# The first feed-forward of a streaming encoder layer by one level of Strassen's scheme

## The chip, the core and the metric

The kernel runs on one core of a Trainium2 chip. The metric is the device time of one launch in microseconds. TensorE (PE) multiplies matrices and writes its results to PSUM; VectorE (DVE) and ScalarE (ACT) read PSUM and SBUF; GpSimd (POOL) works on SBUF; SyncE (SP) issues nearly all DMA transfers between HBM and SBUF.

## The reference, cut

One layer of an encoder for 1024 + 64 = 1088 tokens of width 1024 (two groups of requests, same weights): feed-forward with half weight, token mixing (gated linear attention and stick-breaking attention), second feed-forward, with a layer norm after each. The change concerns the first line.

```python
D_MODEL, D_FF = 1024, 2816

def swiglu(x, w_in, w_out):
    gate, up = jnp.split(x @ w_in, 2, axis=-1)
    return (jax.nn.silu(gate) * up) @ w_out

h = layer_norm(DN_ALPHA * x + 0.5 * swiglu(x, ffn1_w_in, ffn1_w_out), ln1_g, ln1_b)
...
h = layer_norm(DN_ALPHA * h + mix, ln2_g, ln2_b)
y = layer_norm(DN_ALPHA * h + 0.5 * swiglu(h, ffn2_w_in, ffn2_w_out), ln3_g, ln3_b)
```

All is float32. A product is made as three matmuls of rounded operands: each operand is split into a high part (a cast) and a low part (what the cast left over), and high x high, high x low and low x high are summed in PSUM.

## The kernel before, in words

Activations lie transposed, features on the 128 partitions and tokens along the free axis. The tokens are cut into three chunks of 384, 384 and 320 (`CHUNKS`). The hidden width is 22 tiles of 128 (`NH`), the model width 8 (`KT`).

`stage` (L460 and after) loads x chunk by chunk, two feature tiles per DMA into `xt`, and splits it: ScalarE casts to `X0h`, `X1h`, `X2h` (L467), VectorE subtracts to `X0l` and so on (L468). `ffn` makes the feed-forward. Its `gate_up` takes one hidden tile and for each chunk makes the gate in a bank `mm` and the up product in a bank `up`, 24 matmuls each (`mm3`, L235 to L237); ScalarE applies silu (L314), VectorE multiplies by 0.5 and the up product (L315), ScalarE and VectorE split the result to `hh` and `hl` (L320, L321), which stay in SBUF, five tiles deep. After every four hidden tiles `out_tiles` multiplies them by the output weights (L366 to L368) and VectorE adds the bank to the accumulator `acc` in SBUF (L378; for the first four tiles L371 and L374 start it from x itself). Weights are loaded as 512 KB into `raw` (`wraw`, L173; `wtile`, L206; L347), cast by ScalarE into `wh` (L185) and subtracted by GpSimd into `wl` (L186). `first` puts the first hidden tiles between the loads of x; `middle` alternates four gate/up tiles and four output tiles; `last` keeps gate/up of tiles 18 to 21 and their output for the third chunk.

`layer_norm` (generator) works on a chunk: sums over the feature tiles on VectorE (L251 to L256), the mean by a matmul with `ones` into `st` (L247), differences (L261), squares (L263), the variance in the same way, a square root and a reciprocal (L275), then gain and bias (L277, L280). `norm_split` splits the result for the next matmuls (L291, L293). `finish1` is the norm of a chunk with its store to `d_h`. `weave(main, filler)` takes steps of `filler` (matmul work) between the steps of `main` for as many microseconds as `main` asks: the norms of chunks 0 and 1 are woven with `last`, that of chunk 2 with `gla_early`, the first products of the token mixing for chunks 0 and 1.

The order on each engine is made by the framework's planner from the program order and its own estimate of what is ready; an operation whose operands and buffers are free can move ahead of others. A pool of buffers that lands on the memory of a closed pool waits for all users of that pool. The only other pools in the way here are `hp` and `pf` (hidden tiles and banks of the feed-forward) and `xp`.

## Time and profile before

| what | value |
|---|---|
| median of 3 runs | 3009.25 us (3008.7 to 3011.52) |
| profiled execution, its own time | 3012.4 us |
| span of the profiled execution | 3010.7 us |
| mean granted TensorE clock | 0.993 |
| matmul instructions | 18444 |

The profile is one execution. A matmul's recorded length overlaps that of the next, so the rate of TensorE is read from the distance between starts. Busy shares are given for stretches of the span; the granted clock is 1.0 at the upper of its two levels (2.4 GHz) and 0.5 at the lower (1.2 GHz).

### The profile page before, as it was taken

How to read it: one execution, taken by the hardware profiler on the slowest of the kernel's cores; microseconds unless marked ns; L12 is line 12 of the kernel's file. 1: busy time of each engine (PE TensorE's matmuls, PEld its weight loads, DVE VectorE, ACT ScalarE, POOL GpSimd, SP SyncE). 2: the span in 40 equal slices, each digit the busy share in tenths (PEclk: the TensorE clock that was granted, in tenths of full speed). 3: DMA queues.
4: the chain of work that ended last, by engine and by line, in shares of the span. 5: the costliest groups of instructions: out<-in, count | busy, mean ns of one | idle time of the engine just before them, and what ended most of it. 6: DMA issues, size and time to landing. Idle time of an engine off the chain costs nothing. (4 is left out here: it accounts for less than half of the span.)

```text
span 3010.7 us, 43873 instructions
## 1 busy us (share of the span) xinstructions
PE 2941.7 (98%) x18444; PEld 2887.6 (96%) x18444; DVE 1077.2 (36%) x1715; ACT 885.1 (29%) x1721; POOL 895.1 (30%) x714
## 2 busy tenths in 40 slices
PE   8999999999899999999999999999799999999997
PEld 8999999999788999999999999999799999999997
DVE  2232121223845434334444444253842121212226
ACT  3111111111555433323333333222542111111125
POOL 3212212223632211122223222334754122122225
PEclk9999999999999999999999999999999999999998
DMA  4111111112423121221223223544432111111123
GB/s 138 47 38 50 46 46 42 44 52 61 133 69 71 39 57 54 80 77 51 82 55 91 70 71 105 168 129 133 131 103 85 43 50 38 55 43 42 44 84 109
DMA packets 217302, 220.06 MB, mean 73 GB/s; under 512 B 10160, under 2 KB 214704, under 8 KB 217104
## 3 DMA queue, kind: packets, MB, share of 16 engines
q1 hardware_dynamic: 203280, 199.42, 23.0%
q10 hardware_dynamic: 13824, 17.83, 1.6%
q8 instruction: 145, 2.38, 0.3%
q14 instruction: 53, 0.43, 0.0%
HBM read 180.52 MB, written 36.70 MB: 72 GB/s over the span
## 5 line engine op out<-in xcount | busy, mean ns | idle before, releaser
L186 POOL TENSOR_TENSOR wl<-raw,wh 128x512 fp32r<-128x512 f32 (+1 forms) x498 | 736.9, 1499 | 1760.7 <-ACT wh L185 1750.3
L185 ACT CAST wh<-raw 128x512 fp32r<-128x512 f32 (+1 forms) x498 | 321.5, 675 | 962.4 <-PE up L367 325.2
L315 DVE SCALAR_TENSOR_TENSOR sg<-sg,up 128x384 f32<-128x384 f32 (+1 forms) x132 | 70.2, 532 | 745.1 <-PE up L237 743.5
L235 PE MATMUL mm<-X0h,wh 128*128 128x384 f32 (+1 forms) x864 | 292.9, 339 | 10.8 <-ACT wh L185 10.7
L235 PE MATMUL mm<-X2h,wh 128*128 128x320 f32 (+1 forms) x928 | 296.1, 319 | 5.4 <-DVE g L1025 2.9
L237 PE MATMUL mm<-X2h,wl 128*128 128x320 f32 (+1 forms) x928 | 291.3, 314 | 2.1 <-POOL wl L186 2.1
L237 PE MATMUL mm<-X0h,wl 128*128 128x384 f32 (+1 forms) x864 | 289.5, 335 | 1.6 <-POOL wl L186 1.6
L236 PE MATMUL mm<-X2l,wh 128*128 128x320 f32 (+1 forms) x928 | 291.1, 314 | 0.0
L236 PE MATMUL mm<-X0l,wh 128*128 128x384 f32 (+1 forms) x864 | 289.3, 335 | 0.0
L235 PE MATMUL mm<-X1h,wh 128*128 128x384 f32 x800 | 272.6, 341 | 1.7 <-DVE qs L605 1.7
L237 PE MATMUL mm<-X1h,wl 128*128 128x384 f32 x800 | 268.1, 335 | 0.0
L236 PE MATMUL mm<-X1l,wh 128*128 128x384 f32 x800 | 268.1, 335 | 0.0
L235 PEld LDWEIGHTS mm<-X2h,wh 128*128 128x128 f32 x928 | 175.5, 189 | 8.2 <-ACT wh L185 3.6
L367 PE MATMUL mm<-hl,wh 128*128 128x384 f32 (+1 forms) x528 | 173.7, 329 | 6.0 <-DVE hl L321 6.0
L237 PEld LDWEIGHTS mm<-X2h,wl 128*128 128x128 f32 x928 | 175.3, 189 | 2.4 <-POOL wl L186 2.4
L235 PEld LDWEIGHTS mm<-X0h,wh 128*128 128x128 f32 x864 | 163.2, 189 | 14.2 <-ACT wh L185 11.0
L236 PEld LDWEIGHTS mm<-X2l,wh 128*128 128x128 f32 x928 | 175.6, 189 | 1.0
L368 PE MATMUL mm<-hh,wl 128*128 128x384 f32 (+1 forms) x528 | 173.6, 329 | 0.0
L366 PE MATMUL mm<-hh,wh 128*128 128x384 f32 (+1 forms) x528 | 173.5, 329 | 0.0
L367 PE MATMUL up<-hl,wh 128*128 128x384 f32 (+1 forms) x528 | 172.9, 328 | 0.2
L368 PE MATMUL up<-hh,wl 128*128 128x384 f32 (+1 forms) x528 | 172.9, 327 | 0.0
L366 PE MATMUL up<-hh,wh 128*128 128x384 f32 (+1 forms) x528 | 172.5, 327 | 0.0
(263 smaller groups left out, 6650.3 us busy)
## 6 DMA issues: line engine op xcount, KB each, us to landing
raw<-f_in SPq DMA_DIRECT2D x112, 512.0 KB, 3.6
raw<-w_in SPq DMA_DIRECT2D x70, 512.0 KB, 7.5
raw<-f_out SPq DMA_DIRECT2D x48, 512.0 KB, 4.1
raw<-w_ao SPq DMA_DIRECT2D x16, 512.0 KB, 4.0
raw<-w_bo SPq DMA_DIRECT2D x16, 512.0 KB, 3.7
raw<-w_o SPq DMA_DIRECT2D x16, 512.0 KB, 4.2
v_new<-v SPq DMA_DIRECT2D x4, 1024.0 KB, 4.7
xt<-x SPq DMA_DIRECT2D x8, 384.0 KB, 5.9
```

The lines of the kernel that those rows point to most:

```text
L185: nc.scalar.copy(oh, src)
L186: nc.gpsimd.tensor_tensor(ol, src, f32(oh), op=ALU.subtract)
L235: nc.tensor.matmul(ps[:, :w], wh[:, k, :], xh[:, k, :], start=(k == 0), stop=False)
L236: nc.tensor.matmul(ps[:, :w], wh[:, k, :], xl[:, k, :], start=False, stop=False)
L237: nc.tensor.matmul(ps[:, :w], wl[:, k, :], xh[:, k, :], start=False, stop=(k == KT - 1))
L315: nc.vector.scalar_tensor_tensor(sg, sg, 0.5, psu[:, :w], op0=ALU.mult, op1=ALU.mult)
L366: nc.tensor.matmul(ps[:, :w], wh[:, k, ms], hh, start=(k == 0), stop=False)
L367: nc.tensor.matmul(ps[:, :w], wh[:, k, ms], hl, start=False, stop=False)
L368: nc.tensor.matmul(ps[:, :w], wl[:, k, ms], hh, start=False, stop=(k == n - 1))
```

## The change

The first feed-forward is made with one level of Strassen's scheme in the form with seven products and fifteen sums. In the first half a product is (2 x 2 blocks of weights) by (2 x 2 blocks of x): the weights of one hidden tile are cut by gate/up and by the two halves of the model width; x is cut by those halves and by token halves. Tokens are now 4 x 272 (`HW`), two pairs `c`. For each hidden tile and pair `c` seven products of 4 x 3 matmuls of 272 columns take the place of eight. `weight_forms` makes the seven combined weights of a hidden tile (four sums on VectorE, seven casts on ScalarE, seven subtractions on GpSimd or VectorE), `token_forms` the seven combinations of x once at the start (`make_x`, on VectorE for the first pair, on GpSimd for the second); they stay in SBUF in `xa` and `xb`. The sums over products are made partly in PSUM (bank `qa` collects products 0, 2, 4, 5; `qb` the others) and partly at the evacuation.

The gated activations no longer stay in SBUF. After each pair of hidden tiles `hidden_forms` makes their seven combinations, splits them and stores them to HBM (`d_hc`, 557 KB each). When all 22 tiles are done, the buffers `p1` are closed, an accumulator for all tokens takes their place and is filled with x by four DMAs, and the output half runs over groups of hidden pairs (`GROUPS`), loading the combinations of a group into `xa` or `xb` while the other is used. The output is again seven products, each evacuated by VectorE into one block of the accumulator. The last group runs one token pair after the other; its last four steps are woven with the layer norm of tokens 0 to 543 (in parts of 384 and 160), and the norms of the parts 224 and 320 with the first products of the token mixing for chunk 0 alone. `gla_constants` come later, and the weights of the first feed-forward are laid out on the host so that each load is contiguous. Pools are opened later than before, and with `reuse_waits="tile"`: a tile waits for the users of earlier tiles on its own bytes alone.

The diff, cut to its core:

```diff
     def open_pool(name, **kw):
-        pool = tc.tile_pool(name=name, bufs=1, **kw)
+        pool = tc.tile_pool(name=name, bufs=1, reuse_waits="tile", **kw)
...
+    def weight_forms(A, n, pool, on_pool):
+        def form(src, i):
+            wh = pool.tile([P, 4, P], F32R, name="wh", tag="wh", bufs=7)[:, :n, :]
+            wl = pool.tile([P, 4, P], F32R, name="wl", tag="wl", bufs=7)[:, :n, :]
+            nc.scalar.copy(wh, src)
+            eng = nc.gpsimd if i in on_pool else nc.vector
+            eng.tensor_tensor(wl, src, f32(wh), op=ALU.subtract)
+            return wh, wl
+        def add(a, b):
+            t = pool.tile([P, 4, P], F32, name="sm", tag="sm", bufs=3)[:, :n, :]
+            nc.vector.tensor_tensor(t, a, b, op=ALU.add)
+            return t
+        a11, a12, a21, a22 = A
+        yield form(a11, 0)
+        yield form(a12, 1)
+        s1 = add(a21, a22)
+        s2 = add(a11, s1)
+        yield form(s2, 2)
+        yield form(s1, 3)
+        yield form(add(a11, a21), 4)
+        yield form(a22, 5)
+        yield form(add(a12, s2), 6)
+
+    def token_forms(B, form, neg, add, sub):
+        b11, b12, b21, b22 = B
+        form(0, b11)
+        form(1, b21)
+        n1 = sub(b11, b12)
+        t2 = add(b22, n1)
+        neg(2, t2)
+        form(3, n1)
+        form(4, sub(b22, b12))
+        form(5, sub(t2, b21))
+        form(6, b22)
+
+    def seven(forms, xs, cs, A, B, evac, want=None):
+        for i in range(NPROD):
+            wh, wl = next(forms)
+            bank = A if i in (0, 2, 4, 5) else B(i)
+            fresh = i in (0, 1, 3)
+            for c in cs:
+                x = xs(i, c)
+                n = len(x)
+                for k, (xh, xl) in enumerate(x):
+                    o = bank[:, c, :HW]
+                    nc.tensor.matmul(o, wh[:, k, :], xh, start=(fresh and k == 0), stop=False, **kw)
+                    nc.tensor.matmul(o, wh[:, k, :], xl, start=False, stop=False, **kw)
+                    nc.tensor.matmul(o, wl[:, k, :], xh, start=False, stop=(k == n - 1), **kw)
+            for c in cs:
+                evac(i, c, bank[:, c, :HW])
+            yield cost(3 * n * len(cs), HW)
...
+    def gate_up(j, cs, forms):
...
+        def evac(i, c, ps):
+            if i == 0:
+                nc.scalar.copy(s1[:, c, :], ps)
+            elif i == 1:
+                nc.vector.tensor_tensor(g1[:, c, :], s1[:, c, :], ps, op=ALU.add)
+                nc.scalar.activation(g1[:, c, :], g1[:, c, :], AF.Silu)
+            elif i == 2:
+                nc.scalar.copy(u2[:, c, :], ps)
+            elif i == 4:
+                nc.scalar.copy(u3[:, c, :], ps)
+                nc.vector.tensor_tensor(v[:, c, :], u3[:, c, :], b(6)[:, c, :HW], op=ALU.add)
+            elif i == 5:
+                nc.vector.scalar_tensor_tensor(
+                    h[:, 0, c, :], g1[:, c, :], -0.5, ps, op0=ALU.mult, op1=ALU.mult
+                )
+            elif i == 6:
+                nc.vector.tensor_tensor(g2[:, c, :], u2[:, c, :], ps, op=ALU.add)
+                nc.scalar.activation(g2[:, c, :], g2[:, c, :], AF.Silu)
+                nc.vector.scalar_tensor_tensor(
+                    h[:, 1, c, :], v[:, c, :], -0.5, g2[:, c, :], op0=ALU.mult, op1=ALU.mult
+                )
...
+    def hidden_forms(p):
...
+        def out(i, src, negate):
+            st = big(F32R).rearrange("p (h w) -> p h w", h=2)
+            if negate:
+                nc.scalar.mul(st[:, 0, :], src, -1.0)
+                nc.vector.scalar_tensor_tensor(
+                    st[:, 1, :], src, -1.0, f32(st[:, 0, :]), op0=ALU.mult, op1=ALU.subtract
+                )
+            else:
+                nc.scalar.copy(st[:, 0, :], src)
+                nc.gpsimd.tensor_tensor(st[:, 1, :], src, f32(st[:, 0, :]), op=ALU.subtract)
+            nc.sync.dma_start(out=d_hc[p][:, i].rearrange("p h c w -> p h (c w)"), in_=f32(st))
...
+    make_x(0, B0, nc.vector)
+    for c in range(2):
+        for j in FIRST:
+            forms = weight_forms(w0 if (c, j) == (0, 0) else load_gate_up(j), 4, ws,
+                                 (0, 1, 2, 3, 4, 5, 6) if c == 0 else (0, 1, 5))
+            if (c, j) == (0, 0):
+                for got in load_x(1):
+                    B1 = got
+            drain(gate_up(j, (c,), forms))
+            if (c, j) == (0, 0):
+                make_x(1, B1, nc.gpsimd)
+    hidden_forms(0)
...
+    forms = ahead(all_forms(js, lambda j: 4, load_gate_up, (0, 1, 5)), 5)
+    for j in js:
+        drain(gate_up(j, (0, 1), forms))
+        if j % 2:
+            hidden_forms(j // 2)
+    p1_close()
+    acp, acp_close = open_pool("acp", side="right")
+    acc = acp.tile([P, KT, T], F32, name="acc")
+    for m in range(0, KT, 2):
+        nc.sync.dma_start(out=acc[:, m : m + 2, :], in_=x[m * P : (m + 2) * P, :].rearrange("(k p) w -> p k w", p=P))
...
+    def out_tile(g, mp, cs, tiles, forms):
...
+        def evac(i, c, ps):
+            if i == 0:
+                onto(at(m, c, 0), ps, ALU.add, scale)
+            elif i == 1:
+                onto(at(m, c, 0), ps, ALU.add)
...
+    last = len(GROUPS) - 1
+    steps = [(g, mp, (0, 1)) for g in range(last) for mp in range(4)]
+    steps += [(last, mp, (c,)) for c in range(2) for mp in range(4)]
+    groups = {0: load_group(0)}
+    def outs(steps):
+        for g, mp, cs in steps:
+            if mp == 0 and g + 1 <= last and g + 1 not in groups:
+                groups[g + 1] = load_group(g + 1)
+            yield from out_tile(g, mp, cs, groups[g], oforms)
+    drain(outs(steps[:-4]))
...
+    fill = outs(steps[-4:])
+    weave(chain(norm1(0, 384, nothing, (6.0, 7.0)), norm1(384, 160, nothing, (4.0, 4.0))), fill)
     drain(fill)
...
+    weave(chain(norm1(544, 224, emit1(544, 224), (3.0, 6.0)), norm1(768, 320, emit1(768, 320), (3.0, 6.0))), fill)
```

## Rows read from the trace of the kernel before

**Rows 1.** The page: busy microseconds, share of the span and instructions of each engine.

```profile
PE 2941.7 (98%) x18444; PEld 2887.6 (96%) x18444; DVE 1077.2 (36%) x1715; ACT 885.1 (29%) x1721; POOL 895.1 (30%) x714
```

**Rows 2.** The page's 40 slices: granted clock in tenths, and GB/s moved.

```profile
PEclk9999999999999999999999999999999999999998
...
GB/s 138 47 38 50 46 46 42 44 52 61 133 69 71 39 57 54 80 77 51 82 55 91 70 71 105 168 129 133 131 103 85 43 50 38 55 43 42 44 84 109
```

**Rows 3.** Stretches: length, busy us and instructions by engine, clock, DMA, GB/s.

```profile
10.70:17.20 6.50, 6.13 (x18) 5.62 (x19) 3.45 (x2) 5.15 (x8) 5.71 (x4) 1.00 1.10 341
17.20:750.00 732.80, 732.72 (x4420) 732.40 (x4419) 177.04 (x294) 134.29 (x244) 172.39 (x115) 1.00 0.17 51
750.00:786.00 36.00, 34.08 (x219) 32.76 (x218) 26.88 (x40) 18.45 (x36) 25.96 (x19) 1.00 0.34 102
786.00:814.00 28.00, 20.79 (x112) 19.57 (x111) 24.70 (x26) 16.99 (x28) 17.34 (x11) 0.82 0.42 124
814.00:914.00 100.00, 90.72 (x570) 83.08 (x569) 52.62 (x96) 57.12 (x102) 46.70 (x35) 0.97 0.36 96
```

**Rows 4.** The stretch of the first feed-forward's matmuls as one, same columns.

```profile
10.72:814.05 803.33, 793.77 (x4762) 790.40 (x4763) 232.12 (x359) 174.86 (x314) 221.46 (x147) 0.99 0.19 58
```

**Rows 5.** TensorE in order of time (start, length): runs of three widths, first and last.

```profile
700.46 0.33 PE L235 MATMUL up<-X1h,wh 128*128 128x384 f32 x1
...
708.26 0.33 PE L235 MATMUL mm<-X0h,wh 128*128 128x384 f32 x1
...
778.20 0.31 PE L235 MATMUL mm<-X2h,wh 128*128 128x320 f32 x1
...
781.13 0.31 PE L237 MATMUL mm<-X2h,wl 128*128 128x320 f32 x1
...
831.78 0.28 PE L446 MATMUL mm<-wh,X0h 128*128 128x256 f32 x1
...
835.62 0.28 PE L448 MATMUL mm<-wl,X0h 128*128 128x256 f32 x1
```

**Rows 6.** Groups by shape: count, busy us, mean ns of one, idle time before them.

```profile
L186 POOL TENSOR_TENSOR wl<-raw,wh 128x512 fp32r<-128x512 f32 x432 | 576.9, 1357 | 1288.5 <-ACT wh L185 1278.1 <-PE mm L237 9.5 <-PE st L247 0.3
L186 POOL TENSOR_TENSOR wl<-raw,wh 128x1024 fp32r<-128x1024 f32 x66 | 160.1, 2426 | 472.2 <-ACT wh L185 472.2
L378 DVE SCALAR_TENSOR_TENSOR acc<-acc,up 128x384 f32<-128x384 f32 x88 | 48.7, 553 | 99.1 <-PE up L368 99.1
L843 DVE TENSOR_TENSOR w<-w,kneg 128x1023 f32<-128x1023 f32 x8 | 9.8, 1226 | 0.8
L858 DVE COPY wT<-tr 128x256 f32<-128x256 f32 x16 | 6.7, 420 | 12.2 <-PE tr L852 12.2
L275 DVE RECIPROCAL r<-r 128x384 f32<-128x384 f32 x4 | 10.2, 2540 | 0.0
```

**Rows 7.** VectorE and GpSimd in order of time: start, length, operation.

```profile
134.19 2.42 DVE L321 TENSOR_TENSOR hl<-sg,hh 128x320 fp32r<-128x320 f32 x1 [0.78 <-ACT hh L320]
...
133.88 2.39 POOL L186 TENSOR_TENSOR wl<-raw,wh 128x1024 fp32r<-128x1024 f32 x1 [1.11 <-ACT wh L185]
...
805.84 0.48 DVE L378 SCALAR_TENSOR_TENSOR acc<-acc,up 128x320 f32<-128x320 f32 x1
806.23 0.48 DVE L378 SCALAR_TENSOR_TENSOR acc<-acc,mm 128x320 f32<-128x320 f32 x1
```

**Rows 8.** The first microseconds in order of time.

```profile
0.80 1.98 SPq L464 DMA_DIRECT2D xt<-x  x4
...
4.20 0.83 ACT L467 CAST X0h<-xt 128x768 fp32r<-128x768 f32 x1 [2.12 <-DMA xt<-x]
...
10.72 0.69 PE L235 MATMUL mm<-X0h,wh 128*128 128x384 f32 x1 [10.72 <-ACT wh L185]
```

**Rows 9.** DMA issues: count, KB each, median us from issue to landing.

```profile
raw<-f_in SPq DMA_DIRECT2D x112, 512.0 KB, 3.6
...
y<-yX0l SPq DMA_DIRECT2D x3, 512.0 KB, 2.6
```

More of the change, by code (lines that the diff above doesn't have):

```diff
@@ L114, in tile_encoder_layer @@
     d_gb = dr.tile([D, T], F32, name="d_gb")
+    d_hc = [dr.tile([P, 7, 2, 2, HW], F32, name=f"d_hc{p}") for p in range(NP)]
     ident = cp.tile([P, P], F32, name="ident")
@@ L473, in tile_encoder_layer @@
[L473 to L487 removed]
+    NPROD = 7
+    def weight_forms(A, n, pool, on_pool):
[20 more added lines that the diff above has]
+        yield form(add(a12, s2), 6)
```

306 lines of the change are left out of this document (243 added, 63 removed).

## The prediction

> **What bounds the kernel now.** I read the page's busy times first: TensorE is busy for 98% of the span, VectorE for 36%, GpSimd for 30% [rows 1]. The slices say that this holds nearly everywhere: the granted clock is full except at the end [rows 2]. Then the stretches of the first feed-forward [rows 3]: it has its first matmul at 10.7 us, runs without a gap from 17 to 750 us, and loses time only around the first layer norm (20.8 of 28 us busy between 786 and 814 us, granted clock 0.82). Its last matmul ends at 814.0 us. So the way to shorten it is fewer or cheaper matmul columns, and what matters of every addition is whether it makes TensorE wait. A busy share is not a rate, so I took the rate from the distance between starts in long runs [rows 5]: 45 matmuls of 384 columns in 7.80 us are 173.3 ns each, 20 of 320 columns in 2.93 us 146.5 ns, 32 of 256 columns in 3.84 us 120 ns. All three are columns / 2.4 plus 13.3 ns. Hence 272 columns cost 126.7 ns.
>
> **The matmuls.** Before: 22 hidden tiles x 2 x 8 x 3 for gate and up, and 22 x 8 x 3 for the output, are 1584 per token chunk; two chunks of 384 and one of 320 give 1584 x (173.3 + 173.3 + 146.5) ns = 781.1 us in 4752 matmuls (the stretch has 4762 with the norm's [rows 4]). After: 22 tiles x 7 products x 4 x 3 x 2 = 3696, and 4 output pairs x 7 x 11 hidden pairs x 3 x 2 = 1848, together 5544 of 272 columns, 702.4 us. The saving is 78.7 us, not the 97.6 us that an eighth of 781.1 would be, since there are 792 more matmuls of 13.3 ns fixed cost, and shorter ones. The Trainium skill (TensorE: Matmul & The Clock Gate, Wait — 56ns, not 53.3ns?) gives a fixed cost of about 2.5 ns for a warm matmul. By that the saving would be 87.8 us; the three widths above say 13.3 ns, so the sum does not use it.
>
> Against these 79 us stand stalls that the old order did not have. I go through the new first stretch stage by stage and compare its sum with 814.0 us.
>
> **Start, four half tiles.** All of GpSimd's operations take two SBUF inputs, and so do the splits and sums on VectorE. Rows 7 show that such a pair does not run side by side: a split of 320 columns on VectorE took 2.42 us where its like takes about half a microsecond, and it ended 0.34 us after the GpSimd operation that was running. An evacuation that reads PSUM is not held up (the mean of 88 stays at 553 ns [rows 6]). The Trainium skill (SBUF — State Buffer, Who interferes with whom) states this as an exclusive lock of a shared port pair; the trace agrees, with the 2.42 us, and it speaks against this change, which gives both engines far more of such work.
> Prices [rows 6]: GpSimd 1.36 us for 512 columns and 2.43 for 1024, so about 2.56 for 1088, 1.42 for 544, 0.82 for 256. VectorE 1.23 us for 1023 columns, thus 1.3 for 1088 and 0.69 for 512; queued behind one another they start about 0.09 us earlier (320 columns each 0.40 instead of 0.49 us [rows 7]), so 1.2, 0.60, 0.33 (256) and, from 553 ns for 384 columns, 0.35 for an evacuation of 272.
> In the start GpSimd makes 14 weight splits (19.0 us) and ten operations of 1088 columns for the second half of x (25.6); VectorE makes eight sums (4.8) and 12 operations of 1088 columns (14.4). One after the other that is 63.8 us, starting when x arrives: the old x lands at 4.2 us [rows 8], the new first block is 557 KB and lands at about 5. If nothing overlaps, the second half's operands are complete at 69 us. After that TensorE has the last product of one half tile and one whole half tile, 12 us, plus about 3 us at the lower clock level: between 10.7 and 17.2 us the old kernel placed 18 matmuls [rows 3], where 37 fit at full clock. That is 84 us for 42.6 us of matmul time. Ends: 72 if a quarter of the port work overlaps, 98 if the second half's loads, which wait for six buffers, come late.
>
> **The other 20 gate/up tiles.** 20 x 168 x 126.7 ns = 425.7 us. One tile takes TensorE 21.3 us. Beside it VectorE has eight weight operations (4.8), two SBUF products (0.7), half of the pair's five hidden operations (1.6) and eight evacuations (2.8): 9.9 us; GpSimd has three weight splits and half of six hidden ones: 8.3. Even if each GpSimd operation stopped VectorE for its whole length, 18.2 is under 21.3, so this work is covered; if that cover were gone, each microsecond over 21.3 would count 20 times. A bank of PSUM is needed again one or two products (3 us each) after its evacuation was asked for. I take 429 us; ends 426 and 441 (0.75 us a tile). HBM traffic is 6.0 MB per 42.6 us, 141 GB/s, where 341 GB/s was moved between 10.7 and 17.2 us [rows 3]: hidden.
>
> **Between the halves.** The accumulators take the memory of the activations' buffers and start with x, so the first evacuation waits for the last hidden forms to be stored, then for a load. After the last gate/up matmul: silu and products about 1.6 us, then three GpSimd forms, about 7 us to the last store's issue. By then SyncE has issued the loads of the first two groups (3.9 and 7.8 MB, each tile when its last reader has gone, from 20 us before), 1.0 MB of weights and 3.9 MB of stores; the accumulators' first load is 1.1 MB. That is 17.7 MB through one queue. 512 KB rows of 4 KB land 2.6 us after issue, rows of 1 KB after 3.6 [rows 9], so rows of 4.35 KB should move faster than the 341 GB/s, which were made with rows of 1 and 1.5 KB; with an estimate of 400 the first load lands about 44 us after minus 20 plus a latency of 2: TensorE waits about 26 us, and nothing covers it, since evacuation is next on the same PSUM bank. Ends: 14 (store, then load, with the queue empty) and 45 (300 GB/s, and all four loads awaited).
>
> **The output half.** Group 0 has one hidden pair: per output pair TensorE needs 42 x 126.7 = 5.3 us, VectorE 14 evacuations and seven small operations (0.2), 6.3 us: VectorE sets the pace, 25 us for four (21 to 33). Groups 1 to 4: TensorE 84 x 126.7 = 10.64 us, VectorE 14 x 0.35 + 7 x 0.33 = 7.2, GpSimd 4 x 0.82 = 3.3; VectorE is covered even when stopped by all of GpSimd's. What remains is the one place where a product follows the one before it on the same bank (the sixth after the fifth): about 0.25 us each. 16 x 10.64 + 4 = 174 us (171 to 186). Group 5 runs by halves: 5.3 us per step plus 0.6 us at that place, 24 us for the first four (22 to 27). HBM gives 9.9 MB per 43 us: hidden.
>
> **The last four steps with the layer norm.** TensorE has 21.3 us and statistics. VectorE has 19 us for the steps; for the norm of 384 tokens 18 operations of about 0.47, a reciprocal of 2.54 [rows 6] and eight of 0.53, 15 us; for the first half of the norm of 160 tokens about 4. So 38 us, VectorE being the pace (30 to 48). Old: from 750 us on, 64 us with 55 us of TensorE work [rows 3].
>
> **The sum.** 84 + 429 + 26 + 25 + 174 + 24 + 38 = 800 us against 814.0: 14 us less. Behind it both kernels do the same: 100 us with 90.7 us busy [rows 3] before. After, only one chunk is ready to fill the norm of the other 544 tokens (VectorE some 35 us, TensorE 29 us of work before it needs the next chunk); I take 1 us more (-3 to +10). The closer waits on reused memory can gain little: after 914 us the clock stays full to the end region [rows 2]. The net is -13 us: 3012.4 us of the profiled execution (span 3010.7) become 2999.4. The median of the runs shown, 3009.25, is 3.15 us below the profiled execution, so the forecast is 2996 us.
>
> **Rivals.** (1) The stalls are smaller: GpSimd's and VectorE's start overlaps, and the hand-over is near its lower end. For it: VectorE's evacuations need no turn and can fill the waits; against it: the 2.42 us of rows 7. 72 instead of 84, 14 instead of 26, and 5 us less at the norm: 29 us less, 2967. Chance 0.18. (2) Slower: the hand-over decides. Everything that SyncE issued in the 20 us before the seam stands ahead of the load that the first evacuation waits for. At 300 GB/s, and with all 4.4 MB awaited, it costs 45 us and not 26, and the start comes near its upper end, 95: 30 us more than forecast, 3026. It decides from a wait of 39 us at the seam, or the same 13 us in the start. For it: the load can't be issued before the last store has been made; against it: the larger rows. Chance 0.30. (3) It is no change: gain and stalls cancel within 6 us, 3009. Chance 0.12. (4) The fixed cost per matmul disappears in the new order, so that 272 columns cost 272 / 2.4: 5544 x 13.3 ns = 74 us less, 2922. The same weights serve two matmuls in a row as before, and all three widths of rows 5 have the 13.3 ns: 0.02, counted as faster. (The Trainium skill's figure, cited above, would come near it.) That the scheme saves no matmul time is excluded by its count.
>
> **How the numbers follow.** The forecast, 2996, has 0.38. A measurement of this kernel can tell about 0.2%, 6 us. Faster: 0.38 + 0.18 + 0.02 = 0.58; within 0.2%: 0.12; slower: 0.30. If all ends met, the sum would lie between -58 and +64 us; I leave out one in ten on each side: 2960 to 3042. The forecast's own range is 2980 to 3003.
>
> **What would show it.** Matmuls of 272 columns 126.7 ns apart in the middle of the gate/up tiles; the 20 tiles in 426 to 441 us; a hole of 14 to 45 us in TensorE ended by an accumulator load; about 40 us of TensorE idle before 90 us, with GpSimd busy; output pairs of 10.6 us. The forecast fails if VectorE's queue, delayed by GpSimd, sets the pace of the gate/up tiles, or if the seam costs over 39 us.

## The result and the profile after

The changed kernel takes 3077.35 us (median, 3073.85 to 3079.21) where the kernel before takes 3010.02 in the same comparison: a ratio of 1.022 (95% interval 1.020 to 1.024). It is slower by 67 us; forecast were 13 us less. The profiled execution took 3076.39 us.

First the page of the changed kernel, busy times and the slices of clock and GB/s, against [rows 1, 2]:

```profile
PE 2908.0 (95%) x19240; PEld 2829.9 (92%) x19240; DVE 1408.5 (46%) x2429; ACT 1038.9 (34%) x2145; POOL 1023.0 (33%) x866
...
PEclk8999999899979999999999999999999999999998
...
GB/s 120 128 136 151 144 121 168 345 178 224 54 111 61 55 42 54 52 108 53 85 57 80 51 81 73 191 110 128 155 105 90 48 42 42 49 49 42 42 83 106
```

TensorE is busy for 34 us less and the span is 64 us longer: its idle time has grown by 98 us. The clock, full until the end region before, now falls in the first slice, in the eighth and in the twelfth; the first seven slices move 120 to 168 GB/s, and the one with the seam, the border between the two halves of the feed-forward, 345. The same stages as in the forecast, as stretches (columns as in [rows 3]; the last one reaches to the first matmul of the gated attention, which stood at 914.4 us before):

```profile
6.70:33.70 27.00, 17.69 (x84) 15.39 (x85) 24.69 (x19) 14.86 (x21) 17.32 (x10) 1.00 0.70 222
33.70:75.30 41.60, 17.75 (x86) 16.38 (x85) 25.43 (x17) 13.51 (x22) 36.91 (x18) 0.67 0.12 38
75.30:101.90 26.60, 23.77 (x171) 22.76 (x170) 20.15 (x29) 12.26 (x25) 9.56 (x7) 0.94 0.30 104
101.90:544.00 442.10, 432.14 (x3363) 425.02 (x3362) 255.95 (x409) 188.09 (x412) 172.19 (x122) 1.00 0.40 145
544.00:592.40 48.40, 26.65 (x171) 23.58 (x170) 29.46 (x80) 9.95 (x31) 13.59 (x20) 0.79 0.87 330
592.40:780.70 188.30, 177.53 (x1347) 172.50 (x1346) 132.78 (x345) 44.94 (x116) 48.59 (x65) 0.98 0.56 214
780.70:807.00 26.30, 23.37 (x171) 21.75 (x170) 25.06 (x61) 11.21 (x29) 13.79 (x17) 1.00 0.28 80
807.00:850.50 43.50, 31.61 (x176) 27.72 (x175) 38.10 (x91) 21.11 (x49) 17.47 (x25) 0.83 0.17 52
850.50:974.10 123.60, 97.07 (x584) 86.34 (x582) 72.38 (x131) 71.81 (x143) 64.35 (x58) 0.87 0.48 96
```

In the first row the clock column reads 1.00; but up to 24 us matmuls that follow one another start 0.227 us apart, as they do between 41 and 51 us, where the column reads 0.50, so a part of that stretch ran at the lower level as well. The stretch behind the feed-forward, in the kernel before:

```profile
814.00:914.40 100.40, 91.12 (x572) 83.28 (x570) 52.62 (x96) 57.12 (x102) 47.10 (x35) 0.97 0.36 97
```

The feed-forward ends at 850.5 us instead of 814.0, the stretch behind it takes 123.6 us instead of 100.4, and the rest 4.3 us more. Where TensorE stood is told by its waits; the rows below are, in this order, of the start, the twenty tiles, the seam with groups 0 to 4, and the end (waited for: us in all, times, longest):

```profile
PE qb L516 <- POOL wl L469: 12.7, 2, 6.5
PE qa L514 <- ACT u L623: 12.5, 3, 9.9
...
PE qa L514 <- ACT s L618: 9.3, 10, 1.0
...
PE qa L514 <- DVE acc L770: 20.8, 3, 19.1
PE qa L514 <- ACT wh L467: 6.7, 1, 6.7
...
PE st L242 <- DVE s L251: 14.0, 2, 11.8
PE qa L514 <- DVE acc L768: 9.7, 7, 3.3
```

The matmuls are as forecast: in a quiet stretch 7 starts of 272 columns, from 230.95 to 231.70, lie 0.125 us apart, and a quiet tile of 168, with one short wait in it, takes 21.39 us, 127.3 ns each.

```profile
230.95 0.29 PE L514 MATMUL qa<-xc,wh 128*128 128x272 f32 x1
...
231.70 0.29 PE L514 MATMUL qa<-xc,wh 128*128 128x272 f32 x1
```

So the 78.7 us are there. At the forecast's 126.7 ns the 5544 matmuls need 702.4 of the 843.7 us from the first to the last of them, which leaves 141.3 us in which TensorE waits or runs at the lower clock; before it was 814.05 - 10.72 - 781.1 = 22.2. By stage: start 52.6, tiles 16.4, group 0 27.1, groups 1 to 4 18.0, group 5 5.0, last four steps 22.1. The experiments take these apart.

### The profile page after: what moved, and what is told of

It is laid out like the page before. It is cut to its first block, busy times and chain, and to the rows that moved or that the text cites. A ratio compares the mean times of both kernels' runs of the same rounds, so it can differ in the third digit from the quotient of the medians.

```text
span 3074.7 us, 47634 instructions
## 1 busy us (share of the span) xinstructions
PE 2908.0 (95%) x19240; PEld 2829.9 (92%) x19240; DVE 1408.5 (46%) x2429; ACT 1038.9 (34%) x2145; POOL 1023.0 (33%) x866
## 4 chain that ended last, share of the span: by engine, by line
PE 83%; DVE 7%; POOL 3%; ACT 2%; issue 2%; DMA 1%; SPq 0%; DVEq 0%; POOLq 0%; ACTq 0%
PE mm L231 11%; PE mm L233 11%; PE mm L232 11%; PE qa L514 4%; PE qa L516 3%; PE qa L515 3%; PE up L232 3%; PE up L231 3%; PE up L233 3%; PE av L1238 2%; PE qb L514 2%; PE qb L515 2%; PE qb L516 2%; PE mm L442 2%; PE mm L444 2%; PE mm L443 2%
## 5 line engine op out<-in xcount | busy, mean ns | idle before, releaser
L182 POOL TENSOR_TENSOR wl<-raw,wh 128x512 fp32r<-128x512 f32 (+1 forms) x366 | 535.5, 1483 | 1188.3 <-ACT wh L181 1176.5
L181 ACT CAST wh<-raw 128x512 fp32r<-128x512 f32 (+1 forms) x366 | 233.3, 667 | 642.5 <-PE mm L232 205.6
L514 PE MATMUL qa<-xc,wh 128*128 128x272 f32 x1056 | 323.7, 306 | 80.5 <-DVE acc L770 20.8
L516 PE MATMUL qa<-xc,wl 128*128 128x272 f32 x1056 | 310.5, 294 | 0.7 <-POOL wl L469 0.7
L515 PE MATMUL qa<-xc,wh 128*128 128x272 f32 x1056 | 309.6, 293 | 0.0
L469 POOL TENSOR_TENSOR wl<-raw,wh 128x512 fp32r<-128x512 f32 (+2 forms) x156 | 164.2, 1056 | 425.6 <-ACT wh L467 374.4
L514 PEld LDWEIGHTS qa<-xc,wh 128*128 128x128 f32 x1056 | 203.8, 193 | 101.4 <-DVE acc L768 24.8
L516 PE MATMUL qb<-xc,wl 128*128 128x272 f32 x792 | 231.7, 293 | 12.7 <-POOL wl L469 12.7
L514 PE MATMUL qb<-xc,wh 128*128 128x272 f32 x792 | 233.5, 295 | 1.1 <-ACT xc L581 0.6
L515 PE MATMUL qb<-xc,wh 128*128 128x272 f32 x792 | 231.4, 292 | 2.8 <-DVE xc L582 2.8
L231 PE MATMUL mm<-X1h,wh 128*128 128x384 f32 x624 | 212.9, 341 | 0.0
L516 PEld LDWEIGHTS qa<-xc,wl 128*128 128x128 f32 x1056 | 204.2, 193 | 1.4 <-POOL wl L469 1.4
L515 PEld LDWEIGHTS qa<-xc,wh 128*128 128x128 f32 x1056 | 204.7, 194 | 0.2 <-DVE xc L582 0.2
```

What stands on the lines that cost most here:

```text
L181: nc.scalar.copy(oh, src)
L182: nc.gpsimd.tensor_tensor(ol, src, f32(oh), op=ALU.subtract)
L231: nc.tensor.matmul(ps[:, :w], wh[:, k, :], xh[:, k, :], start=(k == 0), stop=False)
L469: eng.tensor_tensor(wl, src, f32(wh), op=ALU.subtract)
L514: nc.tensor.matmul(o, wh[:, k, :], xh, start=(fresh and k == 0), stop=False, **kw)
L515: nc.tensor.matmul(o, wh[:, k, :], xl, start=False, stop=False, **kw)
```

## The experiments

Stages in us, from the starts of the matmuls in each trace; "start" is the first four half tiles, "group 5" its first four steps, and "behind" is from the feed-forward's last matmul to the first of the gated attention; in the kernel before, that is 100.7. "Whole" is the median of the runs. In the first row, the matmuls alone at 126.7 ns.

| kernel | whole | start | 20 tiles | group 0 | groups 1-4 | group 5 | last 4 steps | behind |
|---|---|---|---|---|---|---|---|---|
| matmuls alone | | 42.6 | 425.7 | 21.3 | 170.3 | 21.3 | 21.3 | |
| changed | 3077.4 | 95.2 | 442.1 | 48.4 | 188.3 | 26.3 | 43.4 | 123.7 |
| e1 | 3039.2 | 73.7 | 429.4 | 47.9 | 188.4 | 26.3 | 43.5 | 123.1 |
| e2 | 3032.4 | 69.6 | 442.0 | 48.4 | 171.2 | 28.1 | 43.1 | 123.5 |
| e3 | 3062.3 | 95.3 | 427.8 | 48.5 | 188.7 | 26.3 | 44.6 | 123.1 |
| e4 | 3071.6 | 95.3 | 442.1 | 48.5 | 183.3 | 26.3 | 44.3 | 124.2 |
| e5 | 3079.1 | 95.6 | 442.1 | 48.3 | 188.7 | 26.3 | 43.3 | 123.5 |
| e6 | 3074.5 | 93.9 | 442.2 | 48.4 | 188.9 | 26.3 | 42.0 | 123.5 |
| e7 | 3138.3 | 96.3 | 476.5 | 56.1 | 205.5 | 28.6 | 42.6 | 122.7 |
| e9 | 3024.4 | 72.4 | 429.3 | 43.8 | 174.4 | 27.6 | 44.0 | 122.8 |
| e10 | 3041.2 | 95.9 | 442.2 | 48.3 | 188.4 | 25.9 | 28.5 | 103.8 |
| e12 | 3023.3 | 73.7 | 427.7 | 45.4 | 174.6 | 27.7 | 41.4 | 123.1 |
| e13 | 3079.1 | 93.9 | 442.2 | 48.5 | 188.9 | 26.3 | 41.2 | 125.7 |
| e17 | 3030.8 | 76.7 | 429.5 | 47.4 | 170.2 | 29.9 | 45.5 | 122.7 |

**e1: GpSimd out of the gate/up half.** VectorE and GpSimd in order of time in the start of the changed kernel:

```profile
43.94 2.98 DVE L474 TENSOR_TENSOR sm<-raw,sm 128x512 f32<-128x512 f32 x1 [4.82 <-POOL wl L469]
46.95 2.88 DVE L474 TENSOR_TENSOR sm<-raw 128x512 f32<-128x512 f32 x1
...
43.88 2.49 POOL L592 TENSOR_TENSOR big<-big 128x1088 f32<-128x1088 f32 x1
46.34 5.84 POOL L582 TENSOR_TENSOR xc<-big,xc 128x1088 fp32r<-128x1088 f32 x2
```

A sum of 512 columns on VectorE takes 2.9 us, ending each time some 0.6 us behind the end of a GpSimd operation. The Trainium skill (SBUF — State Buffer, Who interferes with whom) calls this an exclusive lock on a shared port pair; the trace agrees, with these 2.9 us against the 0.69 us that the same sums take in e1.

```diff
-(0, 1, 2, 3, 4, 5, 6) if c == 0 else (0, 1, 5)
+()
...
-forms = ahead(all_forms(js, lambda j: 4, load_gate_up, (0, 1, 5)), 5)
+forms = ahead(all_forms(js, lambda j: 4, load_gate_up, ()), 5)
...
-make_x(1, B1, nc.gpsimd)
+make_x(1, B1, nc.vector)
...
-nc.gpsimd.tensor_tensor(st[:, 1, :], src, f32(st[:, 0, :]), op=ALU.subtract)
+nc.vector.tensor_tensor(st[:, 1, :], src, f32(st[:, 0, :]), op=ALU.subtract)
```

> All forms of the first feed-forward's gate/up half (weights, both halves of x, hidden) that were on GpSimd go to VectorE; nothing is left out. Theory (the two engines stop each other on work with two SBUF inputs, and GpSimd takes twice as long for it: 2.43 us for 1024 columns against 1.23): the start, 6.7 to 101.9 us in the changed kernel, shrinks by 15 to 25 us, the twenty gate/up tiles stay at 21.4 and 22.8 us because VectorE's work of about 13.5 us a tile is still under TensorE's 21.3; in all 3050 to 3062 us instead of 3077. Rival (VectorE's queue sets the pace once it has all the work): the start stays at 102 us or grows, the tiles grow over 22 us, and the time is 3077 or more.

3039.2 us, 38 less: more than expected. The start gave 21.5, within the theory; the tiles, which were to stay, gave 12.7, since the even ones lost their stall too. Start and tiles of this run as stretches:

```profile
6.80:80.50 73.70, 58.74 (x336) 54.15 (x337) 68.02 (x97) 41.03 (x67) 0.00 (x0) 0.88 0.43 138
80.50:509.90 429.40, 429.26 (x3363) 424.75 (x3361) 282.70 (x528) 187.35 (x412) 1.84 (x4) 1.00 0.41 149
```

A group of VectorE's operations in its start (count, busy us, mean ns):

```profile
L474 DVE TENSOR_TENSOR sm<-raw,sm 128x512 f32<-128x512 f32 x11 | 7.6, 688 | 0.2
```

The same sums take 0.69 us, one engine does in 282.7 us of the tiles what two did in 428.1, and TensorE has no gap there. What remains of the start is VectorE itself: 68.0 of 73.7 us busy. The edit takes away two things at once, the hold-up of VectorE and the queue of GpSimd itself, which in the changed kernel was busy for 36.9 of the 41.6 us of the second half tile; no run parts them.

**e2: the second half of x left out.**

```diff
-            if (c, j) == (0, 0):
-                for got in load_x(1):
-                    B1 = got
...
-                make_x(1, B1, nc.gpsimd)
+                XC[1] = XC[0]
```

> Leaves out the loading and combining of the second half of x: the second half's products use the first half's operands, so the first feed-forward is computed on wrong tokens, with the same matmuls. Theory (the start is lost to the second half's operands: four loads that wait for buffers, ten GpSimd operations that queue with 14 weight splits): half tiles 27, then 11 to 14 us each, the start ends at about 62 to 70 us instead of 101.9, the whole 3037 to 3047 us. Rival (the first half tile's own loads, splits and the weight splits are the limit): only a few us less in the second half tile, the start ends behind 85 us.

3032.4 us, 45 less. 25.6 us of it are the start, whose second half tile falls from 41.6 to 16.6 us; the theory holds, but the end at 76.4 us is later than it said. The other 17 us came in groups 1 to 4, which it had not expected. Without a second half the memory of group 1's operands is free early: in the trace their loads are issued ahead of the accumulators', two weight blocks instead of one go out before those of group 2, and the first two output pairs take 22.4 instead of 33.8 us. The compiled order of the products is another too (see e7): the later pairs take 10.59 instead of 11.04 us.

**e3: hidden forms spread.** The edit makes `hidden_forms` a generator, advanced by one form behind each product of the next tile.

```diff
-        drain(gate_up(j, (0, 1), forms))
+        for _ in gate_up(j, (0, 1), forms):
+            next(pending[0], None)
```

> The seven hidden forms of a pair of tiles are issued one behind each product of the next tile, instead of all seven ahead of it; nothing is left out. Theory (every second tile loses 1.2 to 1.4 us because its first product's ScalarE copy stands behind the seven ScalarE casts of the hidden forms, which themselves wait for VectorE's sums): the even tiles fall from 22.8 to 21.4 us, the twenty tiles from 442 to 428 us, the whole to about 3063 us. Rival (the stall is VectorE's or GpSimd's, by the shared port, and moves with the work): 442 us stays, with the stall elsewhere in the tile; 3077.

3062.3 us, 15 less, all of it in the tiles: every tile takes 21.3 to 21.4 us. The stall of an even tile, in the changed kernel: a hidden form's cast on ScalarE, the copy queued behind it, and TensorE waiting for that copy.

```profile
152.61 3.43 POOL L656 TENSOR_TENSOR big<-ht,big 128x544 fp32r<-128x544 f32 x2
...
153.12 0.64 ACT L655 CAST big<-ht 128x544 fp32r<-128x544 f32 x1 [0.59 <-issue]
153.67 0.38 ACT L618 COPY s<-qa 128x272 f32<-128x272 f32 x1
...
154.10 0.39 PE L514 MATMUL qa<-xc,wh 128*128 128x272 f32 x1 [0.92 <-ACT s L618]
```

e1 cured the same stall without moving the casts; that GpSimd's share of the forms (3.43 us for two) holds them up in the changed kernel is inferred.

**e4: output weights first.**

```diff
-            if mp == 0 and g + 1 <= last and g + 1 not in groups:
+            if mp == 1 and g + 1 <= last and g + 1 not in groups:
```

> The loads of the next group's hidden operands are issued one output pair later, so that the output weights of the pairs ahead go first; nothing is left out. Theory (at 605 us TensorE waits 6.7 us for the cast of a weight block whose load stood behind 14 operand loads in SyncE's queue, and then runs 7 us at the lower clock): groups 1 to 4 fall from 188 to about 179 us, the whole to about 3068. Rival (the operands of the next group now come too late, or the transfers themselves are the limit, 29.7 MB in 100 us): the gap moves to the first product of the next group, 188 us or more, 3077 or more.

3071.6 us, 6 less where 9 were expected. The 6.7 us gap is gone, and what waits are left in groups 1 to 4 are for VectorE's evacuations:

```profile
PE qa L514 <- DVE acc L768: 5.6, 12, 2.0
```

The first two pairs of group 1 take 27.7 instead of 33.8 us, the third 11.9 instead of 11.0. The theory holds at two thirds of its size.

**e5 and e9: the seam.** e5 divides the accumulators into four tiles; the first lies over the last tile's evacuation buffers.

```diff
-    acc = acp.tile([P, KT, T], F32, name="acc")
+    for i in (3, 2, 0, 1):
+        accs[i] = acp.tile([P, 2, T], F32, name=f"acc{i}", tag=f"acc{i}")
```

> The accumulators become four tiles of two rows of blocks each instead of one tile of eight; the one of the first output pair lies where the last tile's evacuation buffers were, so its load of x needn't wait for the last hidden forms to be stored. Nothing is left out. Theory (the 19.1 us wait between the halves is the order store, then load, of one tile: its load was issued 10.8 us after TensorE had stopped, behind the last store, and landed 8 us later): the gap falls to 4 to 9 us, group 0 from 48.4 to 33 to 39 us, and the whole to 3062 to 3068 us, the lower clock behind the gap becoming shorter with it. Rival (the transfers are the limit: the queue moved 400 GB/s of group loads in front of it): the gap stays over 14 us, and the whole over 3072.

3079.1 us: nothing, as the rival has it (the gap stays, 18.9 us), but not for the rival's reason: the loads had not been issued yet. SyncE's issues in the changed kernel:

```profile
549.18 6.75 SPq L657 DMA_DIRECT2D d_hc<-big  x5
555.98 1.41 SPq L744 DMA_DIRECT2D xc<-d_hc  x2
557.57 2.22 SPq L733 DMA_DIRECT2D acc<-x  x4
```

The five stores each wait for a hidden form, and the loads stand behind them in SyncE's program (558.0 us in e5), whatever memory is free; e9 shows that the first of them could have gone earlier. e9 is e1 with the four tiles, loaded by GpSimd:

```diff
-        nc.sync.dma_start(out=accs[m // 2], ...)
+        nc.gpsimd.dma_start(out=accs[m // 2], ...)
```

> The run without GpSimd in the gate/up half, and on top of it the accumulators in four tiles whose loads of x are issued by GpSimd, which is idle there, instead of SyncE. Nothing is left out. With four tiles alone nothing had changed: SyncE issued the accumulators' loads at 558.0 us, still behind the last pair's stores (last at 556.2). Theory (it is the order in SyncE's queue, not memory or transfer, that makes TensorE wait): the loads go out within 3 us of the last gate/up matmul, the gap falls from 19 to 5 to 9 us, group 0 from 47.9 to 33 to 38 us, the whole from 3039 to 3024 to 3030 us. Rival (the accumulators' memory comes free only with the last stores, or the transfers in front are the limit): the gap stays over 14 us, 3035 or more.

3024.4 us, 15 less than e1. The first load is issued 0.5 us after TensorE has stopped (511.3 us), instead of 10.8 us (546.8):

```profile
511.79 0.87 POOL L742 DMA_DIRECT2D acc<-x  x1 [0.63 <-DVE big L634]
```

and TensorE's waits between 505 and 560 us have a longest of 10.9 instead of 19.1 us:

```profile
PE qa L514 <- DVE acc L779: 14.4, 4, 10.9
```

That load now takes 9.6 us to land (7.3 in the changed kernel), which is most of the wait that is left. The whole came out as expected, the place did not: group 0 gained 4.1 us, to 43.8 where 33 to 38 were expected, and 14.0 us came in groups 1 to 4, where the wait of 6.7 us for weights and the lower clock behind it are gone (SyncE issued three weight blocks from 532 to 540 us, ahead of the next 14 operand loads, where the changed kernel had issued one), and where another compiled order made output pairs of 10.82 us.

**e17: the first accumulator early.** e9, with the first of the four in memory of its own and its load put ahead of the twenty tiles; six instead of seven buffers for the split weights make room for it.

> The run without GpSimd in the gate/up half and with the accumulators' loads issued by GpSimd, and on top of it the first accumulator (two of eight blocks of rows) in memory of its own, loaded with x at the start of the twenty tiles; six instead of seven buffers for the split weights make room. Nothing is left out. Theory (the 11 us gap that is left at the seam is the wait for the first accumulator's memory and load): no gap over 3 us there, the clock stays full, group 0 falls from 43.8 to 28 to 34 us, the whole from 3024 to 3008 to 3014 us. Rival (the second accumulator or the operands come just as late): the gap moves to the second output pair, group 0 stays over 40 us, 3020 or more.

3030.8 us, 6 more than e9: the rival. At the seam TensorE doesn't wait for the first accumulator, but 11.8 us for the second, whose load GpSimd issued at 530.4 us. The first load, which had nothing to wait for, did not go out at the twenty tiles but at 1.6 us, among the first loads of x:

```profile
1.62 0.87 POOL L722 DMA_DIRECT2D acc<-x  x1
...
530.43 2.17 POOL L745 DMA_DIRECT2D acc<-x  x3
```

The start is 4.3 us longer than in e9; whether by this load or by the missing buffer was not tested, so the 6 us are not the seam's alone. The longest wait at the seam:

```profile
PE qa L514 <- DVE acc L782: 13.8, 4, 11.8
```

By these two runs the seam is a whole set of buffers that changes hands, not one load.

**e7: each half evacuated at once.**

```diff
-            for c in cs:
-                evac(i, c, bank[:, c, :HW])
+                evac(i, c, bank[:, c, :HW])     # inside the loop over c
```

> Each token half of a product is evacuated as soon as its own matmuls are done, instead of both behind the second half's matmuls; nothing is left out. Theory (the 0.42 to 0.45 us that each output pair of groups 1 to 4 loses is the sixth product waiting for the fifth one's evacuation in the same bank, which is asked for only when both halves are done): with the first half evacuated beside the second half's matmuls the output pairs fall from 11.04 to 10.6 us, groups 1 to 4 by 7 us, the whole to about 3070. Rival (the wait is the engines' signalling or VectorE's queue, whatever the request): 11.04 stays, 3077.

3138.3 us, 61 more: both sides fell. The compiled program no longer had the same order: matmuls of one product stand between those of another in another bank, so that its waits come in the middle of products: six in the tile that starts at 318.4 us, where a tile of the changed kernel has one or three. A wait costs more than its length: behind it the second matmul starts 0.23 us after the first instead of 0.125.

```profile
321.85 0.29 PE L516 MATMUL qb<-xc,wl 128*128 128x272 f32 x1
322.17 0.39 PE L514 MATMUL qa<-xc,wh 128*128 128x272 f32 x1
322.40 0.29 PE L515 MATMUL qa<-xc,wh 128*128 128x272 f32 x1
322.52 0.29 PE L516 MATMUL qa<-xc,wl 128*128 128x272 f32 x1
```

So whether the 0.42 us at the sixth product (11.04 us for a pair of the changed kernel) is the bank, as forecast, was not tested by this. e2 and e17, whose order also differs, have output pairs of 10.59 us without it.

**e8: six edits at once**, those of e1, e3, e4, e5, e6 and e7.

> The edits of the runs without GpSimd in the gate/up half, with the hidden forms spread, the output weights first, the accumulators in four, no GpSimd around the norm, and each half evacuated at once, all in one kernel; nothing is left out. Theory (each is a separate loss on TensorE's path; only the first two share the 13 us of the even tiles): 38 + 2 + 6 + 12 + 13 + 7 = 78 us less than 3077, about 2999, level with or a little under the kernel before. Rival (a common limit, VectorE or the transfers, stands behind them): the gains don't add, and it stays over 3020.

3088.8 us. It contains e7, and shows its loss (groups 1 to 4 205.4 us); it tells little on the others (its start, 73.5 us, has the gain of e1).

**e6 and e13: the end.** e6 puts GpSimd's splits and sums around the norm on VectorE (`nc.gpsimd` becomes `nc.vector` in `layer_norm`, `split1` and `wsplit` there).

> From the last four output steps to the end of the first layer norm, all that GpSimd did with two SBUF inputs (splits of the normalized tokens and of weights, partial sums) goes to VectorE; nothing is left out. Theory (behind the feed-forward VectorE is held off by GpSimd: sums of 224 columns took 1.29 us and products of 160 to 384 columns 0.74 us in the mean there): the 43.5 us of the last four steps and the 123.6 us behind them shrink by 10 to 18 us together, the whole to 3059 to 3067 us. Rival (what lacks is other work for TensorE beside the norm, and VectorE is already the limit): with more on VectorE the two stretches stay or grow, 3077 or more.

3074.5 us, within 3 of the changed kernel: the theory fell, although its mechanism is in the rows. One group of VectorE's operations behind the feed-forward, of the changed kernel and then of e6:

```profile
L262 DVE TENSOR_TENSOR s<-s,sq 128x224 f32<-128x224 f32 (+1 forms) x8 | 10.3, 1290 | 0.3 <-ACT sq L258 0.2
```

```profile
L263 DVE TENSOR_TENSOR s<-s,sq 128x224 f32<-128x224 f32 (+1 forms) x8 | 3.5, 436 | 0.0
```

Sums fall from 1.29 to 0.44 us, the first matmul on normalized tokens follows 10.1 instead of 15.2 us behind the feed-forward's last, and the stretch is as long as before (123.5 us): what sets its length is not these sums.

e13 makes the norm of tokens 384 to 767 in one piece behind the feed-forward.

```diff
-weave(chain(norm1(0, 384, nothing, (6.0, 7.0)), norm1(384, 160, nothing, (4.0, 4.0))), fill)
+weave(norm1(0, 384, nothing, (6.0, 7.0)), fill)
...
-norm1(544, 224, emit1(544, 224), (3.0, 6.0))
+norm1(384, 384, emit1(384, 384), (3.0, 8.0))
```

> The changed kernel with the norm of tokens 384 to 767 made as one piece behind the feed-forward, instead of 160 of them beside the last four output steps and 224 behind; the split of the first 384 tokens so no longer stands behind the 160's chain on ScalarE and VectorE. Nothing is left out. Theory (the 11.8 us gap at 851 us is the chain of the 160 tokens, with nothing else ready): the last four steps fall from 43.4 to 37 to 40 us, the first matmul on the normalized tokens comes 5 to 9 us behind the feed-forward's last instead of 15, the whole 3062 to 3068 us. Rival (VectorE has the same work in all and is the limit): what is won in front is lost behind, 3072 to 3080.

3079.1 us, the rival: 2.2 us won in the last four steps, 2.0 lost behind.

**e14: gates as filler.** e13 with the sigmoid gates of the first 384 tokens for two weight pairs in the norm's shadow.

> The run above, and on top of it more work for TensorE beside the norm that needs no VectorE evacuation: the sigmoid gates of the first 384 tokens for two weight pairs (taken from later places), ahead of the queries and keys. Nothing is left out. Theory (beside the norm TensorE lacks work that doesn't need VectorE): 5 to 10 us less than the run above. Rival (the weights' splits that it brings along take the shared port from the norm, and the work is only moved): within 4 us of the run above, or more.

3088.4 us, 9 more than e13, as its rival has it. That the weights to split are the reason is the rival's argument, not shown.

**e10 and e11: without the norm.**

```diff
-yield from layer_norm(w, View(t0, w), V_LN1G, V_LN1B, emit, waits)
+yield waits[0]
+yield waits[1]
+for m in range(KT):
+    emit(m)
```

> The changed kernel without the first layer norm: statistics, centring, scaling, and their matmuls are left out, the splits and stores of the tokens stay. Theory (what is lost behind 807 us in the changed kernel is the norm, which no longer has enough other work for TensorE beside it): it takes 35 to 45 us off here, about twice what it takes off the kernel before, so that the difference of the two, 67 us, falls to 40 to 48. Rival (not the norm but what follows the memory's hand-over at the end of the feed-forward costs the time: splits, constants and weights that can't start earlier): it takes off 15 to 25 us here as there, and the difference stays over 58.

> The kernel before without the first layer norm: statistics, centring, scaling and their matmuls are left out, splits and stores stay. The partner of the run above. Theory: 15 to 22 us less than 3010, the gaps and the lower clock between 786 and 814 us and some of the 10 us idle behind it. Rival (the norm is hidden in the kernel before): 5 us or less.

3041.2 us, 36 less than the changed kernel, and 2985.9 us, 26 less than the kernel before in the same comparison (3012.4), where 15 to 22 were expected. The difference falls from 67 to 55 us, between both expectations and nearer to the rival's. Behind the feed-forward, e10 first, then e11:

```profile
836.20:939.80 103.60, 91.70 (x569) 83.98 (x568) 41.45 (x66) 48.18 (x83) 53.68 (x47) 0.93 0.52 102
```

```profile
799.60:887.20 87.60, 85.68 (x570) 79.81 (x568) 21.53 (x54) 39.81 (x62) 33.12 (x24) 1.00 0.33 85
```

With as many matmuls and no norm in either, the changed order takes 16 us more: its gaps sum to 12 us and the clock is 0.93. So of the 23 us behind the feed-forward some 16 are not the norm. By the traces they are the hand-over of memory: the next layer's operands lie over those of the feed-forward. Without the norm the kernel before issues the first two large blocks of the next weights 19.5 us ahead of its last output matmul (799.6 us), the changed kernel 1.4 us ahead (836.0 us), and there the first is cast at 842.9 us. SyncE in e11, then SyncE, ScalarE and GpSimd in e10:

```profile
780.12 3.85 SPq L173 DMA_DIRECT2D raw<-w_in  x2
```

```profile
834.61 2.35 SPq L169 DMA_DIRECT2D raw<-w_in  x2
...
842.90 1.05 ACT L181 CAST wh<-raw 128x1024 fp32r<-128x1024 f32 x1 [4.75 <-DMA raw<-w_in]
...
835.03 7.01 POOL L841 TENSOR_TENSOR X0l<-acc,X0h 128x384 fp32r<-128x384 f32 x7
...
845.89 2.34 POOL L182 TENSOR_TENSOR wl<-raw,wh 128x1024 fp32r<-128x1024 f32 x1
```

GpSimd's own order, token splits ahead of the first weights, is a second reading of the same rows. No run tested either. The other 7 us are the norm, more exposed than before (123.7 - 103.8 = 19.9 against 100.7 - 87.6 = 13.1). In front of that it costs both kernels about the same, 14.9 us in the last four steps here and 14.0 there.

**e12: what had helped, together** (e1, e3, e4, e6, e9).

> All edits that took time off, in one kernel: no GpSimd in the gate/up half, the hidden forms spread, the output weights ahead of the next group, accumulators in four with loads issued by GpSimd, no GpSimd around the norm. Nothing is left out. Theory (separate losses on TensorE's path, the even tiles' stall shared by the first two): 38 + 2 + 6 + 12 + 2 = 60 us less than 3077, 3013 to 3021 us, level with the kernel before, because the start (80 us for 43 us of matmuls) and the norm's end stay. Rival (a common limit behind them): over 3028.

3023.3 us (ratio to before 1.004, 1.002 to 1.005), as e9 alone, and between the theory's 3013 to 3021 and the rival's 3028. Its feed-forward ends at 797.0 us, 17 us ahead of the kernel before, and behind it 123.1 us go by instead of 100.7.

**e15: four first tiles.** e9 with `FIRST = (0, 1, 2, 3)`, the second half's operands made behind the second tile, and one more buffer.

> The run without GpSimd in the gate/up half and with the accumulators' loads issued by GpSimd, and on top of it four tiles instead of two on the first half of x before the second half is needed (one more buffer, and the second half's operands made behind the second tile). Nothing is left out. Theory (the start is VectorE's 40 us of operand work with too few matmuls beside it): the end of the first four tiles comes at 104 to 110 us instead of 122.0, the whole falls from 3024 to 3008 to 3014 us. Rival (the loads of x, which wait for buffers, or the lower clock set the start): 118 us or later, 3020 or more.

3020.7 us, the least of all versions that compute the layer (ratio 1.0031, 1.0021 to 1.0041). The first four tiles end at 119.2 us (122.0 in e9), not at 104 to 110, so the rival's bound is met. The rival's mechanism, the loads or the clock, is not what the trace shows: VectorE is busy for 106.8 of the 112.3 us, so the operand work itself, not its place, is the limit.

```profile
6.90:119.20 112.30, 96.56 (x672) 91.89 (x673) 106.79 (x167) 67.23 (x121) 0.00 (x0) 0.92 0.47 159
```

**e16 and e18**: e15 with e13, e14 and e6; e17 with e3, e4 and e6.

> The run with four first tiles, and the norm by chunks, with gates as filler, and without GpSimd around the norm. Nothing is left out. Theory (the saving of 79 us of matmul time is real, and what hid it were these waits): 3024 - 14 at the start - 15 to 20 at the end, 2988 to 2998 us, faster than the kernel before by 0.4 to 0.7%. Rival (a common limit, VectorE, behind them): 3008 or more.

> The run above with the hidden forms spread, the output weights ahead of the next group, and no GpSimd around the norm. Nothing is left out. Theory (the waits add, and what stays is the start and the end of the norm): 3006 to 3012 us, level with the kernel before. Rival (the three edits do nothing once the others are in, as in the combined run): as the run above, within 4 us.

3028.8 and 3026.4 us, where the theories had 2988 to 2998 and 3006 to 3012. No version that computes the layer reached the kernel before.

## Why the prediction failed, step by step

The matmuls, the seam and VectorE's share were right; the sign came out wrong by four terms that were too small: the start (by 18 us), the twenty tiles (13), groups 1 to 4 (14) and the stretch behind (22). In three of them the prediction had counted how much work an engine has, but not which queue the operand that TensorE needs next stands in. Its stages sum to 800, measured are 850.5 us; behind them it had +1, measured +23, and 0 for the rest, measured +4.3 (not explained). Together that is the 77 us between 2999.4 and 3076.4. Neither of the two signs of failure that it named came: VectorE did not set the pace of the tiles, and the seam stayed under 39 us.

- **The matmuls** (78.7 us saved): right, 127.3 ns where 126.7 was said, 125 in the quiet run above. The fixed cost per matmul did not go away.
- **Start** (84, measured 101.9). The form work did end as said, at 67.1 instead of 69 us. The step that failed is that by then only "the last product of one half tile and one whole half tile" are left for TensorE. It had not kept up: the second half tile ended at 75.3 us, and two more followed in 26.6 us, partly at the lower clock. In the second half tile TensorE waited 6.5 and 6.2 us for weight splits that stood in GpSimd's queue among the operand work, and 9.9 us for a PSUM copy that stood in ScalarE's queue behind a cast which waited for GpSimd's sum:

```profile
59.35 1.10 ACT L581 CAST xc<-big 128x1088 fp32r<-128x1088 f32 x1 [2.23 <-POOL big L592]
60.35 0.38 ACT L623 COPY u<-qa 128x272 f32<-128x272 f32 x1
```

  That the second half's operand work is the cause, e1 (21.5 us) and e2 (25.6 us) show.
- **Twenty tiles** (429, measured 442.1, upper end 441). "A bank of PSUM is needed again one or two products (3 us each) after its evacuation was asked for" left out that the copy stands in ScalarE's queue behind the casts of the hidden forms: e3, 14 us. VectorE's share was right: with all the work of both engines on VectorE the tiles take 429.4 us (e1).
- **Seam and group 0** (26 + 25, measured 48.4): right in sum, the gap being 19.1. The reason given, transfers in one queue, was half of it: 10.8 us went by before the load was issued, behind SyncE's stores, and 7.3 until it landed (e9). The upper end of 45 us does not follow from its own terms: all four loads make 21.0 MB, which at 300 GB/s, minus 20 and plus 2, are 52 us.
- **Groups 1 to 4** (174, measured 188.3): the 0.25 us at the sixth product was 0.42, 3 us in all; what had no term is the 14 operand loads that stand in front of the weights, 6.7 us and the lower clock behind it (e4 won 5 us of it, e9 more, but with another compiled order).
- **Group 5 and the last four steps** (24 and 38, measured 26.3 and 43.4): within their ranges, 2 and 5 us over the terms.
- **Behind the feed-forward** (+1, measured +23). "Both kernels do the same" is the costliest sentence: the same work, but with little ready at its start. The ends given, -3 to +10, had no term for a hand-over of memory without cover. Some 16 of the 23 us are not the norm (e10, e11), some 7 are the norm's; that the 16 are the hand-over is read from the traces, not tested.
- **The rival on the slower side** had the seam as its mechanism and 45 us as its price, and the start as its other sign. The seam stayed under the 39 us from which it decides; the start met its condition, with 18 us over the forecast where it asks for 13. But its 3026 us is 51 short: what made the kernel slower was five places of 5 to 22 us each, in the same direction.

## What to carry to other kernels

A scheme that saves matmuls pays with element-wise work and with phases that hand memory to each other; price every phase border by what is ready on the other side of it, and not only by how much work there is. For each product that TensorE needs next, look up which queue holds its operand (GpSimd's, ScalarE's, SyncE's) and what stands in front there: three of the losses here were an operand behind other work in an engine's order, and most of the wait for the weights went away by moving one line (e4). Work with two SBUF inputs on GpSimd isn't free help for VectorE: in the gate/up half all of it on VectorE alone was 38 us faster (e1), around the norm it made no clear difference (e6).

## What the runs showed of the hardware

- A matmul that waited costs beyond the wait: the next one starts 0.23 us later instead of 0.125 (272 columns). In the changed kernel's feed-forward this holds for all 26 waits of over 0.3 us at the upper clock (0.227 to 0.235 us).
- At the lower clock matmuls of 272 columns start 0.227 us apart instead of 0.125, less than twice as far (changed kernel, 41 to 51 us).
- VectorE's sums of 512 columns took 2.9 us beside GpSimd and 0.69 without it; removing GpSimd took the summed busy time of both in the twenty tiles from 428.1 to 284.5 us.
- The clock stood at its lower level for part of the stretches in which TensorE was idle for long: 0.67 in the mean between 33.7 and 75.3 us (17.75 of 41.6 us busy), 0.79 around the seam; with the gaps between 101.9 and 544 us, ten of 0.9 us, it stayed full.
- An edit of when evacuations are issued moved TensorE's own order, and the kernel took 61 us more (e7): after an edit the compiled order has to be read before its time is put down to the edit.
